# Sums of the MLP's weight factors made early, and the SSD scores masked and summed in PSUM

## The chip, the cores and the metric

The kernel runs on one core of a Trainium2 chip. The metric is the device time of one execution in microseconds (us); three runs of the kernel before gave 3295.22, 3295.41 and 3297.82 us. PE is the matrix engine (TensorE), DVE the vector engine, ACT the scalar engine, POOL the GpSimd engine, SP the engine that only issues transfers. PSUM is the memory that PE writes its products to (eight banks of 512 float32 columns here), SBUF the working memory.

## The reference, cut to what matters

One layer over 2048 tokens plus 16 learned ones, 1024 wide, float32:

```python
z, xbc, dt_raw, u_s5, gates = split(rmsnorm(h) @ w_in)
y_a = ssd_branch(z, xbc, dt_raw, ...)     # scores = C B^T, masked, times decay, times x
y_b = s5_branch(u_s5, ...)                # scan, then y @ w_glu, val * sigmoid(gate)
h = h + (sigmoid(g_a) * y_a + sigmoid(g_b) * y_b) @ w_out
h = h + square(relu(rmsnorm(h) @ w_ff_in)) @ w_ff_out
out = rmsnorm(h)
```

The change touches the inner product of `ssd_branch` (the scores, their mask and the sum over a chunk) and the weights of the two MLP products.

## The kernel before, in words

Every float32 product is made of three matmuls on numbers split into a high and a low part (`mm3`, lines 240 to 246: high x high, high x low, low x high). A split is one ACT copy and one subtraction on DVE or POOL.

**Mixers.** Four blocks of 512 tokens (`b` = 0 to 3). A block has an SSD stage (four groups of four chunks of 128 tokens, beside the dense products that feed them; in block 0 also the S5 scan) and then a tail: the gate products, four GLU groups of two weight units each and two output groups of four units each (`rhs_group`, 16 units in all). In block 0 a unit is loaded raw (512 KB, `wst`), split and written to memory (1 MB, `wsd`); the later blocks load the finished 1 MB units (`wu<-wsd`) on POOL's queue, with three buffers. A group keeps four PSUM banks (`pd`), one for each 128 tokens; DVE empties them (lines 1265 to 1267 in the GLU, 1300 in the output), and only then does PE reuse them. In the trace GLU and output products run from 583 to 685, from 965 to 1065, from 1344 to 1444 and from 1732 on, in block 3 with the MLP's first preparations between GLU (to 1780) and output.

**One chunk of the SSD stage.** `Ssd.front` makes the scores `psc` (three matmuls), masks them into an SBUF tile `smask` (line 836), multiplies the decays `csb` by them (line 838) and splits the result into `mh` and `ml`. `Ssd.back` multiplies `mh` by the high and low halves of `xhl` in one matmul of 128 columns (line 852) and `ml` by the high half in one of 64 (line 854), for each of four heads; DVE adds the two sets of columns with two instructions (line 863). There are 64 such chunks.

**MLP.** Tokens go in three blocks (768, 768, 512). Both products use a Strassen form with seven factors: four sums are made of the four quarters of each pair of raw weight units, and the sums and three quarters themselves are split. There are 32 such groups (8 `di` x 4). In the first block `Weights.make` does all of it: per group two raw loads of 512 KB, four sums on POOL (lines 1369 to 1372, 1383 to 1386), seven splits (`weight`, lines 1344 and 1345: ACT copy, DVE or POOL subtraction) into `wc` tiles, of which there are three, and seven stores of 512 KB to `wcd` on SP (line 1346). The two later blocks only load the finished factors from `wcd`. The first block's products are recorded from 1840 to 2427, the second's from 2440 on.

The order on each engine is planned from a simulated timeline; `tc.issue_after(mm)` keeps instructions from being put ahead of the matmul `mm`. Each engine and each queue then works strictly in its planned order.

Of the kernel before, what the change touches and what calls it, by code (L numbers as in the profile page):

```python
# [9 lines left out]
F32 = mybir.dt.float32  # L10
F32R = mybir.dt.float32r
AF = mybir.ActivationFunctionType
ALU = mybir.AluOpType
# [23 lines left out]
NWC = 5  # L37
NWU = 3
NJK = 1
AHEAD = 1  # L40
NRAW = 4
FPACE = 2
# [85 lines left out]
def _body(ctx, tc, d, out):  # L128
# [63 lines left out]
    tabd = dr.tile([P, NQ, 2, KA + 1], F32, name="tabd")  # L192
    h2d = dr.tile([SEQ, D], F32, name="h2d")
    xtd = dr.tile([7, P, 4, FB[1][1] // 2], F32, name="xtd")
    wcd = dr.tile([8 * 28, P, D], F32, name="wcd")
    csd = dr.tile([NB, NC4 * NH, P], F32, name="csd")
    ud = dr.tile([NM + SEQ, 512], F32, name="ud")
# [51 lines left out]
    def row_scale(ss, rs, n, L=P):  # L249

        V.tensor_scalar(ss[:L, :n], ss[:L, :n], 1.0 / D, EPS, op0=ALU.mult, op1=ALU.add)
        G.tensor_tensor(rs[:L, :n], ss[:L, :n], mhalf[:L, :n], op=ALU.pow)  # L252
# [522 lines left out]
    class Ssd:  # L775
# [47 lines left out]
        def front(self, c):  # L823

            pl, sd, g, x = self.pl, self.sd, self.g, self.ck[c]
            x.cs_ = cs_ = slice(sd.t0 + c * P, sd.t0 + (c + 1) * P)
            self.inputs(x, self.dts, c * NH + g * 4, cs_, P)
            x.dx = pl.tile([P, 4, 64], F32, name="dx", tag="dx", bufs=2)
            V.tensor_tensor(x.dx, x.pth, drow[:, g * 4:g * 4 + 4].unsqueeze(2).broadcast_to([P, 4, 64]), op=ALU.mult)
            x.xhl = pl.tile([P, 4, 2, 64], F32R, name="xhl", tag="xhl", bufs=2)  # L830
            S.copy(x.xhl[:, :, 0, :], x.xdt)
            G.tensor_tensor(x.xhl[:, :, 1, :], x.xdt, x.xhl[:, :, 0, :].bitcast(F32), op=ALU.subtract)
            psc = bank("psc")
            mm3(psc[:, 0:P], sd.bh[:, cs_], sd.bl[:, cs_], sd.ch[:, cs_], sd.cl[:, cs_], True, True)
            sm = pl.tile([P, P], F32, name="smask", tag="smask", bufs=2)
            V.tensor_tensor(sm, psc[:, 0:P], tri, op=ALU.mult)
            csb = self.dec[:, c]
            V.tensor_tensor(csb, csb, sm.unsqueeze(1).broadcast_to([P, 4, P]), op=ALU.mult)
            x.mh = pl.tile([P, 4, P], F32R, name="mh", tag="mh", bufs=2)
            x.ml = pl.tile([P, 4, P], F32R, name="ml", tag="ml", bufs=2)  # L840
            S.copy(x.mh, csb)
            V.tensor_tensor(x.ml, csb, x.mh.bitcast(F32), op=ALU.subtract)

        def back(self, c):

            pl, sd, g, x, dts = self.pl, self.sd, self.g, self.ck[c], self.dts
            i0, cs_ = c * NH + g * 4, x.cs_
            py, po = bank("py"), bank("pyo")
            mm3(po[:, 0:256], sd.ch[:, cs_], sd.cl[:, cs_], self.hh, self.hl, True, True)
            pyv = py.rearrange("p (h a q) -> p h a q", h=4, a=2)  # L850
            for h in range(4):
                T.matmul(pyv[:, h].rearrange("p a q -> p (a q)"), x.mh[:, h, :],
                         x.xhl[:, h].rearrange("p a q -> p (a q)"), start=True, stop=False)
                T.matmul(pyv[:, h, 0, :], x.ml[:, h, :], x.xhl[:, h, 0, :], start=False, stop=True)
            self.update(x, sd.bth[:, c, :], sd.btl[:, c, :], dts.cd, i0, P)
            if c < NC4 - 1:
                self.split()
            x.y = y = pl.tile([P, 4, 64], F32, name="y_", tag="y_", bufs=2)
            for h in range(4):
                V.scalar_tensor_tensor(y[:, h, :], po[:, h * 64:h * 64 + 64], dts.E[:, i0 + h:i0 + h + 1],  # L860
                                       x.dx[:, h, :], op0=ALU.mult, op1=ALU.add)
            for a in range(2):
                V.tensor_tensor(y, y, pyv[:, :, a, :], op=ALU.add)

        def gate(self, c):

# [13 lines left out]
    def decays(pl, dts, g, b):  # L880

        t = pl.tile([P, NC4, 4, P], F32, name="csb", tag="csb", bufs=2 if b else 1)
        src = csd[b].rearrange("(c h) l -> c h l", h=NH)[:, g * 4:g * 4 + 4, :]
        nc.sync.dma_start(t, src.unsqueeze(0).broadcast_to([P, NC4, 4, P]))
        for c in range(NC4):
            for h in range(4):
                i = c * NH + g * 4 + h
                V.tensor_scalar(t[:, c, h, :], t[:, c, h, :], dts.cs[:, i:i + 1], 0.0, op0=ALU.subtract, op1=ALU.min)
        S.activation(t, t, AF.Exp)
        return t  # L890


    xp = pool("xn", stack=xp_st)
# [195 lines left out]
    for b in range(NB):  # L1089
# [166 lines left out]
            xn = make_xn(gp, b + 1, xp)  # L1256
        mh = gp.tile([P, 8, TB], F32R, name="mixh")
        ml = gp.tile([P, 8, TB], F32R, name="mixl")
        for q in range(4):
            n = q // 2  # L1260

            def evac_glu(c, p):
# [4 lines left out]
                V.scalar_tensor_tensor(th, sgbs[n][:, c, o:o + 256], 1.0, th, op0=ALU.add, op1=ALU.mult)  # L1267
                ma = mixA[:, c, q * 256:(q + 1) * 256]
                G.tensor_tensor(ma, ma, th, op=ALU.add)
            rhs_group([(b, U_GLU + q * 2 + i) for i in range(2)], y5h, y5l, evac_glu)  # L1270
            if q % 2 == 0:
                continue
            for c in range(NC4):
# [6 lines left out]
                S.activation(oh, pv, AF.Copy, scale=0.25)  # L1280
                V.scalar_tensor_tensor(ol, pv, 0.25, oh.bitcast(F32), op0=ALU.mult, op1=ALU.subtract)
        if b == NB - 1:
            y5_st.close()
            mp_st.close()
            xp_st.close()
# [9 lines left out]
        for n in range(2):  # L1295
            def evac_out(c, p, n=n, b=b):
# [5 lines left out]
                jk = gp.tile([P, 512], F32, name="jk", tag="jk", bufs=2)  # L1302
                i = b * NC4 + c
                S.activation(jk, xr, AF.Square, accum_out=ssh[:, n, i:i + 1])
            rhs_group([(b, U_OUT + n * 4 + i) for i in range(4)], mh, ml, evac_out)
        if b < NB - 1:
            V.tensor_tensor(ssh[:, 0, b * NC4:(b + 1) * NC4], ssh[:, 0, b * NC4:(b + 1) * NC4],
                            ssh[:, 1, b * NC4:(b + 1) * NC4], op=ALU.add)
            row_scale(ssh[:, 0, b * NC4:(b + 1) * NC4], rsh[:, b * NC4:(b + 1) * NC4], NC4)
        g_st.close()  # L1310
        if b < NB - 1:
            y5_st.close()
# [13 lines left out]
    class Weights:  # L1326
# [14 lines left out]
        def weight(self, w, eng, n, i):  # L1341

            t = wcs[0].tile([P, 2, n, 512 // n], F32R, name="wc", tag="wc", bufs=wcs[1])
            S.copy(t[:, 0], w)
            (V if eng == "v" else G).tensor_tensor(t[:, 1], w, t[:, 0].bitcast(F32), op=ALU.subtract)  # L1345
            nc.sync.dma_start(wcd[i], t.rearrange("p a k n -> p (a k n)").bitcast(F32))
            return t

        def read(self):
# [6 lines left out]
                    yield t.rearrange("p (a k n) -> p a k n", a=2, k=4 if j < 14 else 2)  # L1356

        def make(self):
            for di in range(ND):
                for half in range(2):  # L1360
                    c = 2 * di + half
                    wa, wb = ff_raw(fw, "w1a"), ff_raw(fw, "w1b")
                    nc.sync.dma_start(wa, d["w"][U_FFI + 2 * c])
                    nc.sync.dma_start(wb, d["w"][U_FFI + 2 * c + 1])
                    a11, a12, a21, a22 = [x.rearrange("p (a k n) -> p a k n", a=2, k=4)[:, i]
                                          for x in (wa, wb) for i in range(2)]
                    s2, s3, s1, s4 = [ff_sum(fw, nm).rearrange("p (k n) -> p k n", k=4)
                                      for nm in ("s2", "s3", "s1", "s4")]
                    G.tensor_tensor(s1, a21, a22, op=ALU.add)
                    G.tensor_tensor(s2, s1, a11, op=ALU.subtract)  # L1370
                    G.tensor_tensor(s3, a11, a21, op=ALU.subtract)
                    G.tensor_tensor(s4, a12, s2, op=ALU.subtract)
                    for j, (w, e) in enumerate(zip((a11, s2, s3, a12, s1, a22, s4), ENG[half])):
                        yield self.weight(w, e, 4, di * 28 + half * 7 + j)
                for n in range(2):
                    b1, b2 = ff_raw(fw, "w2a"), ff_raw(fw, "w2b")
                    nc.sync.dma_start(b1, d["w"][U_FFO + 4 * di + n])
                    nc.sync.dma_start(b2, d["w"][U_FFO + 4 * di + 2 + n])
                    b11, b12, b21, b22 = [x.rearrange("p (k a n) -> p k a n", k=2, a=2)[:, :, i, :]
                                          for x in (b1, b2) for i in range(2)]  # L1380
                    t3, t1, t2, t4 = [ff_sum(fw, nm).rearrange("p (k n) -> p k n", k=2)
                                      for nm in ("t3", "t1", "t2", "t4")]
                    G.tensor_tensor(t3, b22, b12, op=ALU.subtract)
                    G.tensor_tensor(t1, b12, b11, op=ALU.subtract)
                    G.tensor_tensor(t2, b22, t1, op=ALU.subtract)
                    G.tensor_tensor(t4, b21, t2, op=ALU.subtract)
                    for j, (w, e) in enumerate(zip((b11, t3, b21, t4, t1, t2, b22), ENG[2 + n])):
                        yield self.weight(w, e, 2, di * 28 + 14 + n * 7 + j)

        def take(self):  # L1390
            ahead = AHEAD if wcs[0] is fw and self.n == 0 else NRAW + wcs[1] - 2
# [373 lines left out]
```

## Time and profile before

| | before |
|---|---|
| median of 3 runs | 3295.41 us |
| profiled execution | 3295.92 us (span 3294.2) |
| PE busy | 3079.3 us (93%) |
| DVE busy | 2082.6 us (63%) |
| POOL busy | 1423.9 us (43%) |
| ACT busy | 1224.1 us (37%) |
| granted clock, mean | 0.97 |
| moved by DMA | 782.9 MB, 238 GB/s |

"Busy" is the share of the span in which an engine had an instruction at work. The granted clock is PE's, as a share of 2.4 GHz. A wait is charged to what came last.

### The profile page before, as it was taken

The page shows a single profiled execution, that of the slowest core. Times are in us where ns is not written, and L with a number is a line of the kernel's source. Part 1 is how long each engine was busy: PE and PEld are TensorE (multiplying, and loading weights), DVE is VectorE, ACT ScalarE, POOL GpSimd, SP SyncE. Part 2 cuts the span into 40 slices and gives each one's busy share as a digit, 9 for nine tenths or more (in the row PEclk, how much of TensorE's full clock was granted, in tenths as well). Part 3 has the DMA queues.
Part 4 walks back from the last instruction along what each step waited for, and adds up shares of the span by engine and source line. Part 5 has one row for each costly group of instructions (what it writes and reads, how often), then busy time and mean ns, then how long its engine had stood idle before and what let it go on. Part 6 is the DMA issues. An engine that isn't in the chain of part 4 may idle for free. (4 is left out here: it accounts for less than half of the span.)

```text
span 3294.2 us, 49794 instructions
## 1 busy us (share of the span) xinstructions
PE 3079.3 (93%) x18353; PEld 2749.2 (83%) x18353; DVE 2082.6 (63%) x4153; ACT 1224.1 (37%) x2428; POOL 1423.9 (43%) x1736
## 2 busy tenths in 40 slices
PE   7898999999999999998999899998879999989998
PEld 6687888877887778877888798888879999989998
DVE  8969997427742576426855566676775555575555
ACT  6254454434431443334433333343442121142222
POOL 4356666524421344213433565656642222243443
PEclk9999999999999999999999899999989999999999
DMA  6486676775556554666756777777788888889998
GB/s 219 146 244 191 198 201 219 271 241 164 168 200 215 185 169 159 209 210 203 233 175 217 271 272 261 264 270 256 271 290 275 247 246 245 249 286 374 358 359 277
DMA packets 297875, 782.90 MB, mean 238 GB/s; under 512 B 90688, under 2 KB 132800, under 8 KB 268448
## 3 DMA queue, kind: packets, MB, share of 16 engines
q0 software_dynamic: 88832, 411.21, 37.5%
q1 hardware_dynamic: 206192, 367.29, 34.1%
q8 instruction: 146, 2.39, 0.3%
q10 hardware_dynamic: 2608, 1.22, 0.1%
q14 instruction: 97, 0.79, 0.1%
HBM read 563.66 MB, written 218.05 MB: 237 GB/s over the span
## 5 line engine op out<-in xcount | busy, mean ns | idle before, releaser
L1504 DVE TENSOR_TENSOR acc<-acc,p 128x512 f32<-128x512 f32 x330 | 225.8, 684 | 172.7 <-PE p L246 169.9
L244 PE MATMUL pd<-hnh,wc 128*128 128x384 f32 (+1 forms) x896 | 293.9, 329 | 29.1 <-DMA wc<-wcd 20.6
L244 PE MATMUL pd<-wu,xnh 128*128 128x512 f32 x768 | 311.1, 406 | 2.3 <-ACT cacc L749 1.6
L245 PE MATMUL pd<-wu,xnh 128*128 128x512 f32 x768 | 310.6, 404 | 0.0
L246 PE MATMUL pd<-wu,xnl 128*128 128x512 f32 x768 | 309.2, 403 | 0.0
L246 PE MATMUL pd<-hnh,wc 128*128 128x384 f32 (+1 forms) x896 | 291.9, 329 | 13.6 <-DVE wc L1345 12.2
L245 PE MATMUL pd<-hnl,wc 128*128 128x384 f32 (+1 forms) x896 | 292.8, 327 | 0.0
L228 POOL DMA_DIRECT2D wu<-wsd x168 | 96.5, 574 | 369.5 <-PE pd L246 305.4
L1355 POOL DMA_DIRECT2D wr<-wcd x227 | 122.4, 540 | 275.2 <-PE pd L246 137.1
L244 PE MATMUL pd<-xnh,wu 128*128 128x512 f32 (+1 forms) x640 | 232.2, 363 | 8.4 <-DMA wu<-wsd 8.4
L246 PE MATMUL pd<-xnh,wu 128*128 128x512 f32 (+1 forms) x640 | 229.6, 359 | 0.0
L245 PE MATMUL pd<-xnl,wu 128*128 128x512 f32 (+1 forms) x640 | 229.5, 359 | 0.0
L1355 POOL DMA_DIRECT2D wc<-wcd x221 | 118.9, 538 | 252.7 <-PE pd L246 134.4
L244 PEld LDWEIGHTS pd<-hnh,wc 128*128 128x128 f32 x896 | 174.3, 195 | 34.0 <-ACT hnh L993 12.9
L246 PEld LDWEIGHTS pd<-hnh,wc 128*128 128x128 f32 x896 | 174.0, 194 | 19.1 <-DVE wc L1345 15.7
L752 DVE SCALAR_TENSOR_TENSOR cacc<-craw,conv,cacc 128x512 f32<-128x512 f32 (+1 forms) x192 | 173.7, 906 | 23.1 <-ACT cacc L749 14.8
L218 POOL TENSOR_TENSOR wu<-wst,wu 128x1024 fp32r<-128x1024 f32 x56 | 138.3, 2471 | 100.0 <-ACT wu L217 98.6
L244 PEld LDWEIGHTS pd<-wu,xnh 128*128 128x128 f32 x768 | 147.0, 191 | 34.8 <-ACT cacc L749 2.4
L245 PEld LDWEIGHTS pd<-hnl,wc 128*128 128x128 f32 x896 | 174.7, 195 | 0.0
L245 PEld LDWEIGHTS pd<-wu,xnh 128*128 128x128 f32 x768 | 147.2, 192 | 31.7 <-issue 0.2
L246 PEld LDWEIGHTS pd<-wu,xnl 128*128 128x128 f32 x768 | 146.9, 191 | 31.8
L244 PEld LDWEIGHTS pd<-xnh,wu 128*128 128x128 f32 x640 | 125.1, 196 | 25.3 <-ACT cacc L749 3.6
(1016 smaller groups left out, 9910.3 us busy)
## 6 DMA issues: line engine op xcount, KB each, us to landing
wu<-wsd POOLq DMA_DIRECT2D x168, 1024.0 KB, 5.2
wr<-wcd POOLq DMA_DIRECT2D x227, 512.0 KB, 5.0
wcd<-wc SPq DMA_DIRECT2D x224, 512.0 KB, 3.5
wc<-wcd POOLq DMA_DIRECT2D x221, 512.0 KB, 5.3
wsd<-wu SPq DMA_DIRECT2D x56, 1024.0 KB, 5.3
wst<-in_w SPq DMA_DIRECT2D x60, 512.0 KB, 5.7
csb<-csd SPq DMA_DIRECT2D x16, 1024.0 KB, 12.0
xt<-in_x SPq DMA_DIRECT2D x28, 512.0 KB, 4.7
```

Source lines behind the costliest of these rows:

```text
L218: eng.tensor_tensor(t[:, 1], raw, t[:, 0].bitcast(F32), op=ALU.subtract)
L228: nc.gpsimd.dma_start(t, wsd[u - U_XBC])
L244: T.matmul(ps, lh, rh, start=first, stop=False, skip_group_check=open_)
L245: T.matmul(ps, lh, rl, start=False, stop=False, skip_group_check=open_)
L246: return T.matmul(ps, ll, rh, start=False, stop=last, skip_group_check=open_).ins
L752: V.scalar_tensor_tensor(acc[:, :n], raw[:, k:k + n], conv[:, mt, k:k + 1], acc[:, :n], op0=ALU.mult, op1=ALU.add)
L1355: nc.gpsimd.dma_start(t, wcd[di * 28 + j])
L1504: V.tensor_tensor(o, o, pv, op=ALU.add)
```

## The change

In the tail of each mixer block a generator, `ff_early`, takes 9, 9, 9 and 5 of the 32 groups of MLP weights: it loads the two raw units, makes the four sums on DVE and stores them, not split, to a new memory tensor `smd` (256 KB each). `early_step` spreads them over the tail's 16 units (in block 3 over the GLU's 8), behind the last matmul of a unit. `Weights.make` no longer makes sums: it loads them (five buffers) and loads of one raw unit of each pair only the half that it still splits; the next group's raw loads are issued behind the first factor of this one. In the SSD stage the mask is applied in place in PSUM, and the two halves of `x` are accumulated into one set of 64 columns with three matmuls of 64 columns for each head, so that one DVE addition is left.

```diff
+EARLY = (9, 9, 9, 5)
...
-            sm = pl.tile([P, P], F32, name="smask", tag="smask", bufs=2)
-            V.tensor_tensor(sm, psc[:, 0:P], tri, op=ALU.mult)
+            sm = psc[:, 0:P]
+            V.tensor_tensor(sm, sm, tri, op=ALU.mult)
...
-            pyv = py.rearrange("p (h a q) -> p h a q", h=4, a=2)
+            pyv = py[:, 0:256].rearrange("p (h q) -> p h q", h=4)
             for h in range(4):
-                T.matmul(pyv[:, h].rearrange("p a q -> p (a q)"), x.mh[:, h, :],
-                         x.xhl[:, h].rearrange("p a q -> p (a q)"), start=True, stop=False)
-                T.matmul(pyv[:, h, 0, :], x.ml[:, h, :], x.xhl[:, h, 0, :], start=False, stop=True)
+                mm3(pyv[:, h], x.mh[:, h, :], x.ml[:, h, :], x.xhl[:, h, 0, :], x.xhl[:, h, 1, :], True, True)
...
-            for a in range(2):
-                V.tensor_tensor(y, y, pyv[:, :, a, :], op=ALU.add)
+            V.tensor_tensor(y, y, pyv, op=ALU.add)
...
+    def ff_early(pl, groups):
+        def load(g):
+            wa, wb = [pl.tile([P, D], F32, name=nm, tag="er", bufs=2) for nm in ("era", "erb")]
+            ff_load(g, wa, wb)
+            return wa, wb
+        raw = load(groups[0])
+        for n, g in enumerate(groups):
+            v, m = ff_pieces(g, *raw)
+            def room(nm):
+                return pl.tile([P, 512], F32, name=nm, tag="es", bufs=4).rearrange("p (k n) -> p k n", k=m)
+            for j, w in ff_sums(g, v, room, V):
+                nc.sync.dma_start(smd[g * 4 + SUMS[m].index(j)], w.rearrange("p k n -> p (k n)"))
+                if j == (6 if m == 4 else 3) and n + 1 < len(groups):
+                    raw = load(groups[n + 1])
+                yield
...
+        slots = 8 if b == NB - 1 else 16
+        early_n = [0, 0]
+        def early_step(mm):
+            early_n[0] += 1
+            want = -(-early_n[0] * EARLY[b] * 4 // slots)
+            with tc.issue_after(mm):
+                while early_n[1] < want:
+                    early_n[1] += 1
+                    next(early, None)
...
-            rhs_group([(b, U_GLU + q * 2 + i) for i in range(2)], y5h, y5l, evac_glu)
+            rhs_group([(b, U_GLU + q * 2 + i) for i in range(2)], y5h, y5l, evac_glu, step=early_step)
...
-            rhs_group([(b, U_OUT + n * 4 + i) for i in range(4)], mh, ml, evac_out)
+            rhs_group([(b, U_OUT + n * 4 + i) for i in range(4)], mh, ml, evac_out, step=early_step if b < NB - 1 else None)
...
         def make(self):
-                    G.tensor_tensor(s1, a21, a22, op=ALU.add)
-                    G.tensor_tensor(s2, s1, a11, op=ALU.subtract)
-                    G.tensor_tensor(s3, a11, a21, op=ALU.subtract)
-                    G.tensor_tensor(s4, a12, s2, op=ALU.subtract)
...
+            def load_sum():
+                g, k = next(more, (None, 0))
+                if g is not None:
+                    t = ff_sum(fw, "sm")
+                    nc.sync.dma_start(t, smd[g * 4 + k])
+                    sums.append(t)
+            load_raws(0)
+            for _ in range(NSUM):
+                load_sum()
+            for g in range(32):
+                (a11, a12, a21, a22), m = ff_pieces(g, *raws.pop(0))
+                ws = {0: a11, 3: a12, 5: a22} if m == 4 else {0: a11, 2: a21, 6: a22}
+                for j in range(7):
+                    w = ws[j] if j in ws else sums.pop(0).rearrange("p (k n) -> p k n", k=m)
+                    t = self.weight(w, ENG[g % 4][j], m, g * 7 + j)
+                    if j not in ws:
+                        load_sum()
+                    if j == 0 and g < 31:
+                        load_raws(g + 1)
+                    yield t
```

## Rows read from the trace of the kernel before

**Rows 1.** The page's part 2: granted clock and DMA rate in 40 equal slices.
```profile
PEclk9999999999999999999999899999989999999999
GB/s 219 146 244 191 198 201 219 271 241 164 168 200 215 185 169 159 209 210 203 233 175 217 271 272 261 264 270 256 271 290 275 247 246 245 249 286 374 358 359 277
```

**Rows 2.** Busy time by stretch: stretch, length, engines, granted clock, DMA share, GB/s.
```profile
1840.00:2427.00 587.00, 525.36 (x3397) 505.72 (x3396) 405.99 (x564) 234.13 (x431) 353.09 (x260) 0.95 0.74 270
2520.00:2890.00 370.00, 369.13 (x2585) 367.88 (x2584) 201.54 (x346) 76.22 (x151) 104.83 (x186) 1.00 0.81 247
```

**Rows 3.** PE's waits from 1840 to 2427: us in total, times, longest.
```profile
PE p L244 <- DVE acc L1504: 14.0, 7, 2.8
PE pd L246 <- DVE wc L1345: 12.2, 7, 2.1
PE py L244 <- DVE acc L1504: 8.1, 6, 1.4
PE p L245 <- POOL wc L1345: 6.6, 7, 1.9
PE px L244 <- DVE acc L1514: 6.4, 5, 1.5
PE p L244 <- ACT wc L1344: 5.4, 7, 1.4
PE pd L244 <- ACT wc L1344: 4.6, 8, 2.1
```

**Rows 4.** All engines' waits from 1840 to 2427, three of the longest.
```profile
ACT wc L1344 <- DMA wcd<-wc: 115.1, 81, 4.1
POOL t L1383 <- DMA w2b<-in_w: 62.9, 12, 6.8
...
POOL s L1369 <- DMA w1b<-in_w: 32.2, 12, 5.1
```

**Rows 5.** POOL's groups from 1840 to 2427: costliest and last of eight sum lines.
```profile
L1384 POOL TENSOR_TENSOR t<-w2a 128x512 f32<-128x512 f32 x16 | 25.2, 1576 | 0.6 <-DVE wc L1345 0.6
...
L1369 POOL TENSOR_TENSOR s<-w1b 128x512 f32<-128x512 f32 x14 | 18.7, 1338 | 41.3 <-DMA w1b<-in_w 32.2 <-DMA wcd<-wc 5.1 <-DVE acc L1504 4.0
```

**Rows 6.** Busy time by stretch, the tails of blocks 0, 1 and 3.
```profile
583.00:685.00 102.00, 101.33 (x475) 81.14 (x474) 40.66 (x64) 38.45 (x66) 46.85 (x32) 1.00 0.75 270
965.00:1065.00 100.00, 100.00 (x470) 80.40 (x469) 34.65 (x63) 23.99 (x50) 20.64 (x32) 1.00 0.58 199
...
1732.00:1780.00 48.00, 48.00 (x219) 38.50 (x219) 18.06 (x37) 11.66 (x26) 15.28 (x24) 1.00 0.57 197
```

**Rows 7.** Busy time by stretch, twenty of the MLP's last block.
```profile
3000.00:3020.00 20.00, 20.00 (x168) 19.89 (x167) 14.76 (x34) 7.64 (x20) 9.34 (x16) 1.00 1.10 389
```

**Rows 8.** DMA issues, from issue to landing: page's part 6; 2500:2880; 3000:3250.
```profile
wst<-in_w SPq DMA_DIRECT2D x60, 512.0 KB, 5.7
...
wr<-wcd POOLq DMA_DIRECT2D x100, 512.0 KB, 4.5
...
wr<-wcd POOLq DMA_DIRECT2D x76, 512.0 KB, 5.6
```

**Rows 9.** PE in order of time (start, duration): scores, then sums of a chunk.
```profile
774.82 0.28 PE L245 MATMUL psc<-cl,bh 128*128 128x128 f32 x1
774.93 0.27 PE L246 MATMUL psc<-ch,bl 128*128 128x128 f32 x1
775.04 0.45 PE L246 MATMUL pd<-wu,xnl 128*128 128x512 f32 x1
...
812.28 0.31 PE L852 MATMUL py<-xhl,mh 128*128 128x128 f32 x1
812.42 0.25 PE L854 MATMUL py<-xhl,ml 128*128 128x64 f32 x1
812.50 0.30 PE L852 MATMUL py<-xhl,mh 128*128 128x128 f32 x1
```

**Rows 10.** DVE's groups over the span; the last row is a pair of L863 (64 pairs).
```profile
L1504 DVE TENSOR_TENSOR acc<-acc,p 128x512 f32<-128x512 f32 x330 | 225.8, 684 | 172.7 <-PE p L246 169.9 <-DMA out<-acc 0.8 <-DMA acc<-h2d 0.7
L838 DVE TENSOR_TENSOR csb<-csb,smask 128x512 f32<-128x512 f32 x64 | 73.1, 1149 | 1.0
...
L863 DVE TENSOR_TENSOR y__3031<-y__3031,py x2: 404/406/408, 273.6 to 276.4; 128x256 f32<-128x256 f32 x2
```

**Rows 11.** Busy time by stretch, the SSD stages of blocks 0 and 1.
```profile
192.00:565.00 373.00, 345.62 (x2073) 298.38 (x2072) 334.34 (x650) 190.72 (x415) 247.11 (x245) 0.95 0.70 201
765.00:965.00 200.00, 194.55 (x975) 161.78 (x974) 133.72 (x309) 79.91 (x169) 89.26 (x132) 0.98 0.54 176
```

More of the change, by code (lines that the diff above doesn't have):

```diff
@@ L39 @@
 NJK = 1
+EARLY = (9, 9, 9, 5)
+SUMS = {4: (1, 2, 4, 6), 2: (1, 3, 4, 5)}
 AHEAD = 1
@@ L194, in _body @@
     xtd = dr.tile([7, P, 4, FB[1][1] // 2], F32, name="xtd")
+    smd = dr.tile([32 * 4, P, 512], F32, name="smd")
     wcd = dr.tile([8 * 28, P, D], F32, name="wcd")
@@ L890, in decays, with ff_pieces, ff_load, ff_sums @@
         return t
+    def ff_pieces(g, wa, wb):
+        if g % 4 < 2:
+            v = [x.rearrange("p (a k n) -> p a k n", a=2, k=4)[:, i] for x in (wa, wb) for i in range(2)]
+            return v, 4
+        v = [x.rearrange("p (k a n) -> p k a n", k=2, a=2)[:, :, i, :] for x in (wa, wb) for i in range(2)]
+        return v, 2
+    def ff_load(g, wa, wb):
+        di, j = divmod(g, 4)
+        ua, ub = (U_FFI + 4 * di + 2 * j, U_FFI + 4 * di + 2 * j + 1) if j < 2 else \
+            (U_FFO + 4 * di + j - 2, U_FFO + 4 * di + j)
+        nc.sync.dma_start(wa, d["w"][ua])
+        nc.sync.dma_start(wb, d["w"][ub])
+    def ff_sums(g, v, room, eng):
+        a11, a12, a21, a22 = v
+        def tt(nm, x, y, op):
+            o = room(nm)
+            eng.tensor_tensor(o, x, y, op=op)
+            return o
+        if g % 4 < 2:
+            s1 = tt("s1", a21, a22, ALU.add)
+            yield 4, s1
+            s2 = tt("s2", s1, a11, ALU.subtract)
+            yield 1, s2
+            yield 2, tt("s3", a11, a21, ALU.subtract)
+            yield 6, tt("s4", a12, s2, ALU.subtract)
+        else:
+            yield 1, tt("t3", a22, a12, ALU.subtract)
+            t1 = tt("t1", a12, a11, ALU.subtract)
+            yield 4, t1
+            t2 = tt("t2", a22, t1, ALU.subtract)
+            yield 5, t2
+            yield 3, tt("t4", a21, t2, ALU.subtract)
+    def ff_split(t, w, eng, i):
+        S.copy(t[:, 0], w)
+        eng.tensor_tensor(t[:, 1], w, t[:, 0].bitcast(F32), op=ALU.subtract)
+        nc.sync.dma_start(wcd[i], t.rearrange("p a k n -> p (a k n)").bitcast(F32))
+    def ff_early(pl, groups):
[13 more added lines that the diff above has]
+                yield
     xp = pool("xn", stack=xp_st)
@@ L1258, in _body @@
         ml = gp.tile([P, 8, TB], F32R, name="mixl")
+        e_st = ExitStack()
+        g0 = sum(EARLY[:b])
+        early = ff_early(pool("early%d" % b, stack=e_st, side="right"), range(g0, g0 + EARLY[b]))
+        slots = 8 if b == NB - 1 else 16
[7 more added lines that the diff above has]
+                    next(early, None)
         for q in range(4):
@@ L1282, in _body @@
         if b == NB - 1:
+            for _ in early:
+                pass
+            e_st.close()
             y5_st.close()
@@ L1309, in _body @@
             row_scale(ssh[:, 0, b * NC4:(b + 1) * NC4], rsh[:, b * NC4:(b + 1) * NC4], NC4)
+        for _ in early:
+            pass
+        e_st.close()
         g_st.close()
@@ L1343, in weight @@
             t = wcs[0].tile([P, 2, n, 512 // n], F32R, name="wc", tag="wc", bufs=wcs[1])
-            S.copy(t[:, 0], w)
-            (V if eng == "v" else G).tensor_tensor(t[:, 1], w, t[:, 0].bitcast(F32), op=ALU.subtract)
-            nc.sync.dma_start(wcd[i], t.rearrange("p a k n -> p (a k n)").bitcast(F32))
+            ff_split(t, w, V if eng == "v" else G, i)
             return t
@@ L1358, in make @@
         def make(self):
[L1359 to L1368, printed above, removed]
-                    G.tensor_tensor(s1, a21, a22, op=ALU.add)
-                    G.tensor_tensor(s2, s1, a11, op=ALU.subtract)
-                    G.tensor_tensor(s3, a11, a21, op=ALU.subtract)
-                    G.tensor_tensor(s4, a12, s2, op=ALU.subtract)
[L1373 to L1388, printed above, removed]
@@ new lines, in make, with load_raws @@
+            raws, sums = [], []
+            more = ((g, k) for g in range(32) for k in range(4))
+            def load_raws(g):
+                di, j = divmod(g, 4)
+                a, b = [ff_raw(fw, nm) for nm in ("wa", "wb")]
+                if j < 2:
+                    u = U_FFI + 4 * di + 2 * j
+                    nc.sync.dma_start(a, d["w"][u])
+                    nc.sync.dma_start(b[:, 512:], d["w"][u + 1][:, 512:])
+                else:
+                    u = U_FFO + 4 * di + j - 2
+                    nc.sync.dma_start(a.rearrange("p (k a n) -> p k a n", k=2, a=2)[:, :, 0, :],
+                                      d["w"][u].rearrange("p (k a n) -> p k a n", k=2, a=2)[:, :, 0, :])
+                    nc.sync.dma_start(b, d["w"][u + 2])
+                raws.append((a, b))
```

## The prediction

> **What bounds the kernel now.** I read the slices first [rows 1]. PE is at work 93% of the span, so only time in which PE stands still or runs at the lower clock can be won, and every matmul that is added in a full stage is paid. The clock row and the busy times by stretch show where that time lies. In the second MLP block PE is full at clock 1.00; in the first, which does the same products, it is busy 525.4 of 587 us at 0.95 [rows 2]. At the second block's rate (2585 recorded matmuls in 370 us, 6.99 per us) the first's 3397 would take 486 us: it loses 101 us. Of these 587 - 525.4 = 61.6 are idle; a mean of 0.95 means that a tenth of the stretch, some 59 us, ran at 1.2 GHz, which loses 29. The four tails, where the sums go, are the opposite: PE full at clock 1.00, with DVE busy only 35 to 41 of 100 us and 197 to 270 GB/s moving [rows 6]. The SSD stages are nearly full (PE 194.6 of 200 in block 1), but in block 0 DVE is at 90% and PE at 93%, clock 0.95 [rows 11].
>
> Second, the waits in the first MLP block [rows 3, 4]. PE waits for late DVE additions (14.0 + 8.1 + 6.4), for weight splits on DVE (12.2) and POOL (6.6), for ACT's copies (5.4 + 4.6). Behind these stand two things: POOL, whose queue stops for raw loads in front of its sums (62.9 + 32.2 us) while splits lie behind them; and the ring of three `wc` tiles, in which ACT waits 115.1 us, 81 times, until a store to `wcd` has landed. The change takes away the first. It does not touch the second.
>
> **Part 1: the first MLP block.** POOL loses 128 sums of 1.34 to 1.58 us [rows 5], some 181 of its 353 busy us. DVE is helped too: a DVE instruction with two SBUF inputs has a mean of 1149 ns where one with an input in PSUM takes 684 [rows 10], and the difference is best read as waiting for POOL. What goes: the POOL waits (7), half of the DVE waits (12.2 + 28.5 = 41, half because POOL's busy time about halves), together 28; and the clock that goes with them, 29 x 28/62 = 13. That is 41 us. The raw loads are no longer late, since they are issued seven factors (some 17 us) ahead and land in about 6.
>
> What comes: each group reads 256 KB less of two raw units and 1 MB of sums, 0.79 MB more, 25 MB over 32 groups. The block now moves 270 x 587 = 158 MB [rows 2]; 184 MB in 550 us would be 334 GB/s. SP issues four more transfers a group, none of which waits for anything that the store ahead of it hasn't waited for. But loads of 512 KB land in 4.5 us at 247 GB/s and in 5.6 at 361 [rows 8]; 64 GB/s more make about 0.6 us, and each `wc` store in the ring gets that later. On 81 waits this is 49 us of ACT; PE now idles 10 of 115 us on ACT directly and more through DVE's splits, so I charge 7. Net -34. Bounds: at 361 GB/s the 184 MB take 509 us, so no more than -78; if PE feels all 49 us of the ring, +8.
>
> **Part 2: the tails.** Each of 32 groups adds 1.05 MB of loads and 1.05 MB of stores: 18.9 MB in blocks 0 to 2, 10.5 MB in block 3. Now 27.5, 19.9, 20.1 (block 2 is like block 1) and 9.5 MB move there [rows 6], so it becomes 46.4, 38.8, 39.0 and 20.0 MB in 102, 100, 100 and 48 us: 455, 388, 390 and 417 GB/s. The most I see over 20 us is 389 [rows 7]. At that rate the tails need at least 119, 100, 100 and 51 us: +20 in all, the lower bound. The Trainium skill's page DMA: Bandwidth & Descriptors (Specifications) puts the limit of memory for one core at about 358 GB/s; by that rule the lower bound would be +52 (+28, +8, +9, +8), but 389 and 361 GB/s were measured here, so I do not use it.
>
> The upper side is the chain of one group, which has only two raw buffers: loads, sums, stores, and only then the next loads. Two loads: 5.7 us for one [rows 8] and 1.35 more for the second's bytes at 389 GB/s, 7.0. Four sums at 0.69 us (the price of a 512-column addition, rows 10; up to 1.15 beside POOL), 2.8. The stores lie ahead of the next loads in SP's queue, 2.7 us of transfer of which up to 2.1 run beside the sums: 0.6 to 2.7. Together 10.4 to 12.5 us, against 11.1 us that a tail has for one group (9.6 in block 3). With half of the bandwidth taken by the other queue the loads cost 2.7 more and it is 15. DVE works in its planned order, so while it waits for a raw unit it does not empty banks; SP likewise holds `xr` loads and `h2d` stores behind, and in block 0 the raw units of the dense products. I take 12.5, and 14 in block 0, whose own traffic is heavier: 9 x 14 - 102 = 24; twice 9 x 12.5 - 100 = 12.5; 5 x 12.5 - 48 = 14.5; 63.5 us. PE has some 4.5 us in hand in each tail (three quarters of a unit of 6 us) before it needs a bank: 63.5 - 18 = +46. Bounds +20 and, at 15 us a group, 33 + 35 + 35 + 27 - 18 = +112. The sums' DVE time itself (36 x 0.69 = 25 us a tail) fits beside its 35 to 41.
>
> **Part 3: the SSD chunks.** PE gets 12 matmuls of 64 columns for a chunk instead of four of 128 and four of 64. The trace has no run of 64-column matmuls. Start to start, matmuls of 128 columns with changing weights take 0.11 us, and the pair of a 128 and a 64 takes 0.22 (812.28 to 812.50), 0.14 of it behind the 128 and 0.08 behind the 64 [rows 9]. If each costs 0.11 whatever its columns, four more make 0.44 us a chunk, 28 us over 64; if a 64 costs 0.08, three make 0.24 for 0.22, 5 us in all. I take 0.11, since the 0.22 of a pair is twice that. The Trainium skill's page TensorE: Matmul & The Clock Gate (LDWEIGHTS) says that a weight load takes the weights' columns over 1.2 in ns, which for 128 is 107 ns however few columns follow; by that rule it is 27 us, by the cheap reading 5.
>
> DVE loses one addition (0.41) and, with the mask in PSUM, perhaps 1149 - 684 = 0.47 of the multiplication [rows 10]: 0.87 us a chunk. In block 0, where DVE limits, 16 chunks give 14 us for 7 of PE: -7. In the other three 48 x 0.44 = +21 is paid on a nearly full PE, and at best the waits of 5.5 us a block [rows 11] halve: +14 with 7 off. Sum +7, bounds -20 and +25. The masked scores hold their bank some 1.5 us longer; four such banks turn, and I price that at nothing; if a transposition waits for it, it costs up to that per chunk in block 0 alone, 24 us.
>
> **The sum.** -34 + 46 + 7 = +19. The profiled execution took 3295.9, 0.5 above the median of the runs; 3295.4 + 19 = 3314 us.
>
> **Rivals.** (a) Faster: POOL was the root in the first MLP block, the ring was late only through it, and the block comes within 30 us of the second's rate (-70), while the plan hides the chains of the tails down to their bytes (+22): with part 3, -41, 3254 us. For it: 95 us of POOL's waits on raw loads in front of splits. Against: the 115 us of ACT on stores. It decides as soon as the block wins over 53. (b) Part 3 is good: 64-column matmuls are cheap and DVE was the limit: -20 instead of +7, 3287 us, about no change. (c) The change doesn't do what it says: POOL is freed, but the ring of three with later stores keeps the first MLP block where it was: 46 + 7, 3348 us. (d) The tails fall to 15 us a group: 112 + 7 - 34, 3380 us; the clock would then fall there too.
>
> **How the numbers follow.** Forecast 0.38, (a) 0.31, (b) 0.12, (c) 0.13, (d) 0.06. A measurement of this kernel tells 0.2%, 6.6 us, from no change. Faster: (a) and 0.05 of (b), 0.36. Same: 0.05 of (b) and 0.04 from the forecast's edge, 0.09. Slower: 0.55. The cases of both signs are likely; the forecast's own range is 3300 to 3335, and the range that holds 8 in 10 reaches from (a) to (d): 3250 to 3380.
>
> **What would show it.** Part 1: POOL's waits for `w2b` and `w1b` gone, PE busy over 92% and clock above 0.96 in the first MLP block, ACT still waiting for `wcd` stores over 100 us, about 340 GB/s; block some 550 us. Part 2: the tails of 100 us at 110 or more, over 350 GB/s, DVE waiting for `era` or `erb`, PE for DVE in front of `pd`, clock below 1.00. Part 3: eight gaps of 0.9 us become twelve of 1.3; the multiplication near 684 ns. Wrong outright: a first MLP block under 515 us, or tails that stay at 100 us.

## The result and the profile after

The changed kernel takes 3333.15 us (median of four runs, 3326.03 to 3345.93) against 3296.61 for the kernel before in the same comparison: 1.0113 times as long, 95% interval 1.0081 to 1.0145, so 36.5 us slower. The forecast was 3314. The profiled execution is the fastest of the four, 3326.03 us (span 3324.3). The stages below therefore explain 30 us; the other 6 belong to executions that left no trace.

A stage is taken from the first product of one part to the first of the next, in both traces; only the tails of blocks 0 to 2 and the first MLP block end with their own last product. What PE stands still behind such a product counts in the next stage: 3.5 us behind the first tail of the changed kernel, a wait for a `wu` load, are part of the +11.8.

| stage | before, us | after - before, us | forecast |
|---|---|---|---|
| start to the first tail (S5, SSD of block 0) | 583.2 | -2.3 | -7 |
| SSD stages of blocks 1, 2, 3 | 847.5 | +11.8, +3.6, +7.0 | +14 together |
| tails of blocks 0, 1, 2 | 301.0 | +19.7, +17.9, +17.0 | +46 with the next row |
| GLU of block 3 (the last tail) | 47.7 | +4.5 | |
| output of block 3, preparation | 61.0 | -1.9 | 0 |
| first MLP block | 586.3 | -38.3 | -34 |
| the rest | 867.5 | -8.9 | 0 |

The tails cost 59, the SSD stages 20; the MLP gives 38 back, and 9 more at the start of its second block. Page part 2 of after, clock and DMA rate in 40 slices:

```profile
PEclk9999999999999999999999999999999999999999
...
GB/s 218 147 244 193 209 203 229 354 288 192 154 229 317 234 169 159 246 336 235 185 197 255 285 329 339 338 329 327 341 313 291 250 247 247 247 282 373 361 358 278
```

Three tails stand out as new peaks (354, 317, 336), and the first MLP block moved from about 266 to about 333 [rows 1]. The same by stretch (length; busy time of PE, weight load, DVE, ACT, POOL; clock, DMA share, GB/s), for the four tails and the first MLP block of after, then the first tail in thirds:

```profile
581.00:702.00 121.00, 106.68 (x472) 83.35 (x471) 59.14 (x96) 38.07 (x65) 49.18 (x33) 0.94 0.95 366
994.00:1112.00 118.00, 106.51 (x472) 83.46 (x471) 54.21 (x96) 24.50 (x51) 21.71 (x32) 0.96 0.89 311
1395.00:1512.00 117.00, 104.56 (x470) 81.98 (x469) 54.81 (x96) 24.23 (x51) 20.94 (x32) 0.97 0.88 311
1806.00:1859.00 53.00, 51.20 (x225) 40.37 (x224) 25.22 (x52) 12.71 (x27) 15.33 (x23) 0.97 0.91 321
1917.00:2466.00 549.00, 507.24 (x3399) 491.10 (x3399) 350.90 (x566) 234.21 (x433) 184.94 (x140) 0.98 0.93 335
...
581.00:620.00 39.00, 29.80 (x129) 23.68 (x128) 21.59 (x35) 13.44 (x23) 12.22 (x8) 0.82 0.87 324
620.00:660.00 40.00, 40.00 (x191) 31.10 (x190) 26.91 (x47) 15.23 (x29) 23.98 (x18) 1.00 0.98 376
660.00:702.00 42.00, 36.89 (x156) 28.57 (x155) 10.63 (x17) 9.41 (x16) 12.99 (x7) 1.00 1.01 394
```

PE was full at 1.00 in these tails [rows 6]. Now it is idle for 14.3, 11.5, 12.4 and 1.8 us, 40 in all. A mean clock of 0.94 to 0.97 means that 12, 8, 6 and 6% of the stretches ran at 1.2 GHz, 34 us in all. In 7 of these PE stood still anyway, and the other 27 lose half of their time, some 14 us. Together about 54 of the 59 us. DVE stays at half load, so it isn't the engine that is full. The DMA engines nearly are: their share is 0.88 to 0.95 where it was 0.57 to 0.75.

### The profile page after: what moved, and what is told of

It is laid out like the page before. It is cut to its first block, busy times and chain, and to the rows that moved or that the text cites. A ratio compares the mean times of both kernels' runs of the same rounds, so it can differ in the third digit from the quotient of the medians.

```text
span 3324.3 us, 50855 instructions
## 1 busy us (share of the span) xinstructions
PE 3107.3 (93%) x18609; PEld 2770.4 (83%) x18609; DVE 2044.2 (61%) x4217; ACT 1220.6 (37%) x2426; POOL 1220.7 (37%) x1608
## 5 line engine op out<-in xcount | busy, mean ns | idle before, releaser
L247 PE MATMUL pd<-xnh,wu 128*128 128x512 f32 (+1 forms) x640 | 231.2, 362 | 12.3 <-DMA wu<-wsd 12.1
L247 PEld LDWEIGHTS pd<-hnh,wc 128*128 128x128 f32 x896 | 172.0, 192 | 26.3 <-issue 17.0
L755 DVE SCALAR_TENSOR_TENSOR cacc<-craw,conv,cacc 128x512 f32<-128x512 f32 (+1 forms) x192 | 165.7, 865 | 25.9 <-ACT cacc L752 14.7
L247 PEld LDWEIGHTS pd<-xnh,wu 128*128 128x128 f32 x640 | 124.0, 194 | 29.6 <-issue 11.8
```

What stands on the lines that cost most here:

```text
L247: T.matmul(ps, lh, rh, start=first, stop=False, skip_group_check=open_)
L755: V.scalar_tensor_tensor(acc[:, :n], raw[:, k:k + n], conv[:, mt, k:k + 1], acc[:, :n], op0=ALU.mult, op1=ALU.add)
```

## The experiments

Times are medians, ratios are to the kernel before on the same chip with their 95% interval, stage times from the profiled execution against before's.

**1. The three parts apart.** The sums alone are after with the old mask and the old two sets of columns; the other three kernels are before with one or both edits of the SSD chunk:

```diff
-            sm = pl.tile([P, P], F32, name="smask", tag="smask", bufs=2)
-            V.tensor_tensor(sm, psc[:, 0:P], tri, op=ALU.mult)
+            sm = psc[:, 0:P]                            # mask in PSUM
+            V.tensor_tensor(sm, sm, tri, op=ALU.mult)
...
+                mm3(pyv[:, h], x.mh[:, h, :], x.ml[:, h, :], x.xhl[:, h, 0, :], x.xhl[:, h, 1, :], True, True)   # y in one set
...
+            V.tensor_tensor(y, y, pyv, op=ALU.add)
```

> The early sums alone; scores masked into SBUF and y in two sets of columns as before. Theory: the tails cost about 59 us, the first MLP block gives back 38 and what follows 9, and the SSD stages are as before, so 3296 + 12 = 3308 us, SSD stages within 4 us of before. Rival (the 20 us that the SSD stages lost are a spill of the early transfers into them, not the four added matmuls): 3326 us, SSD stages 15 to 20 us longer than before.

> The SSD edits alone, no early sums. Theory: 64 chunks x 0.44 us of matmul is 28 us on PE, less what DVE's relief saves, some 8: 3296 + 20 = 3316 us, with twelve matmuls of 64 columns 0.11 us apart. Rival (spill): PE's added matmuls hide behind waits, no slower than before, 3290 to 3297 us.

> The mask in PSUM alone. Theory: the multiplication falls from 1149 to 690 ns, 29 us of DVE; PE gets nothing more, so only the waits on DVE shrink: -4 to -10 us, 3290 us. Rival (the scores' bank held longer delays PE, or the time of DVE was not on the path): 3296 or some us more.

> y in one set of columns alone: four more matmuls and one DVE addition less for each of 64 chunks. Theory: +28 us of PE, less 26 us of DVE that were mostly beside PE: +20 to +25, 3318 us. Rival (matmuls of 64 columns are cheap or hide): 3290 to 3300 us.

| kernel | us | ratio | stages against before |
|---|---|---|---|
| sums alone | 3322.25 | 1.0087 (1.0063 to 1.0112) | tails and GLU 3 +20.4, +17.2, +22.4, +4.3; output 3 +4.3; MLP -46.9 |
| mask and y | 3311.68 | 1.0053 (1.0034 to 1.0072) | SSD of blocks 0 to 3 -1.6, +8.2, +4.2, +7.8 |
| mask alone | 3283.43 | 0.9971 (0.9957 to 0.9984) | SSD -6.2, -0.6, -3.5, -2.0 |
| y alone | 3315.40 | 1.0070 (1.0048 to 1.0093) | SSD +3.3, +10.0, +5.4, +7.6 |

The parts add up within their intervals: 27 and 17 make 44, measured 36.5. Mask and y came close to what was expected. The sums alone, expected at 3308, cost 14 us more; their profiled execution (3314.88 us) shows half of that, in the tails and the output. Their SSD stages stayed within 6 us of before, so the rival that the early transfers spill into these stages falls. The edits of the chunk have opposite signs. y alone costs 26.3 us in the stages, almost the 28 of its matmuls: the DVE addition that it saves is worth some 2. (The total of y alone is smaller, because its first MLP block, in which nothing was changed, came out 12 us shorter in the profiled execution; one stage of one execution can be off by that much.) The mask alone gains 12.3 in the stages, and it is the best version here, faster than both kernels. Its mechanism is one row, DVE's multiplication with the mask alone (busy us, mean ns | idle before), which was 1149 ns with the mask's product in SBUF [rows 10]:

```profile
L838 DVE TENSOR_TENSOR csb<-csb,psc 128x512 f32<-128x512 f32 x64 | 43.2, 681 | 1.1
```

The single instructions show what the 1149 were made of. Before, the 12 multiplications with no POOL instruction at work beside them took 681 ns in the mean, the other 52 1257; with the mask's product in PSUM it was 680 for 15 and 682 for 49 (the spans on POOL are rough). So this multiplication was slow where POOL worked beside it, and the operand in PSUM took that away.

And PE in order of time (start, duration) in a chunk of after shows the price of 64 columns, which no row of before had:

```profile
799.65 0.28 PE L247 MATMUL py<-xhl,mh 128*128 128x64 f32 x1
799.76 0.28 PE L248 MATMUL py<-xhl,mh 128*128 128x64 f32 x1
799.88 0.28 PE L249 MATMUL py<-xhl,ml 128*128 128x64 f32 x1
799.99 0.28 PE L247 MATMUL py<-xhl,mh 128*128 128x64 f32 x1
```

They start 0.11 us apart, as matmuls of 128 columns do [rows 9]. The Trainium skill's page TensorE: Matmul & The Clock Gate (LDWEIGHTS), which the prediction weighed, gives 107 ns for a weight load of 128 columns by its rule; the trace agrees.

**2. What makes the tails long: the chain of two raw buffers, DVE's sums, or the bytes.** Three kernels, each from the sums alone: four raw buffers of each name with the next group loaded ahead; the raw loads of a tail's first group only (the later sums are made of old data); and no sums on DVE, with the raw pieces stored in their place, so the transfers are the same.

```diff
-            wa, wb = [pl.tile([P, D], F32, name=nm, tag="er", bufs=2) for nm in ("era", "erb")]
+            wa, wb = [pl.tile([P, D], F32, name=nm, tag="er", bufs=4) for nm in ("era", "erb")]
...
-                    raw = load(groups[n + 1])
+                    pass
...
-            for j, w in ff_sums(g, v, room, V):
-                nc.sync.dma_start(smd[g * 4 + SUMS[m].index(j)], w.rearrange("p k n -> p (k n)"))
+            for k, j in enumerate((4, 1, 2, 6) if m == 4 else (1, 4, 5, 3)):
+                w = raw[k // 2][:, (k % 2) * 512:(k % 2) * 512 + 512]
+                nc.sync.dma_start(smd[g * 4 + SUMS[m].index(j)], w)
```

> The early sums alone (as e1_sums_only), with four raw buffers instead of two: a group's raw units are loaded before the sums of the group ahead. Bytes are the same. Chain theory (a tail is paced by load, sums, stores, load): tails fall from 20 us above before to 0 to 8, 3322 - 45 = 3277 us. Rate theory (388 to 455 GB/s are more than the queues give, so buffers do not help): tails stay 15 us or more above, 3312 to 3325 us.

> The early sums alone, but in each tail only the first group's raw units are loaded and summed again for every group: 8 of 9 MB of loads are left out, and with them what a sum waits for; sums and stores stay. Both DMA theories: tails within 5 us of before, 3322 - 55 = 3267 us. Rival (the 36 sums' own time on DVE delays the banks): tails stay 12 us or more above, 3305 us or more.

> The early sums alone, but DVE makes none: quarters of the raw units are stored in place of the sums, so loads, stores and bytes are the same and the sums' values are left out. If the delay reaches PE through DVE standing before a raw unit, tails fall to 0 to 8 us above before, 3280 us. If it reaches PE through the transfers of the dense work (wu, xr, yt late for want of bandwidth or behind on SP's queue), they stay 12 us or more above, 3310 us.

| kernel | us | ratio | tails 0, 1, 2 and GLU 3 against before |
|---|---|---|---|
| sums alone | 3322.25 | 1.0087 (1.0063 to 1.0112) | +20.4, +17.2, +22.4, +4.3 |
| four raw buffers | 3323.83 | 1.0077 (1.0062 to 1.0092) | +25.2, +13.4, +11.7, +2.0 (SSD 3: +17) |
| few raw loads | 3291.91 | 0.9983 (0.9971 to 0.9995) | +18.2, +4.7, +6.0, +7.6 |
| no sums on DVE | 3324.61 | 1.0078 (1.0055 to 1.0101) | +17.5, +14.0, +17.0, +10.4 |

The chain falls: with twice the buffers the total stays, and what tails 1 and 2 and GLU 3 win comes back in SSD 3 and tail 0; tails 1 and 2 still lose 25 of 40 us. DVE falls: without one sum the tails are still 59 us longer. Taking away 8.4 of the 18.9 MB wins tails 1 and 2 nearly back, but not tail 0, and the total misses the expected 3267 by 25 us. By stretch, tails 0 and 1 with few raw loads:

```profile
586.00:706.00 120.00, 107.28 (x473) 83.99 (x471) 67.91 (x97) 38.82 (x67) 52.21 (x33) 0.94 0.84 305
991.00:1095.00 104.00, 100.73 (x468) 80.10 (x467) 54.92 (x96) 23.96 (x51) 22.15 (x32) 1.00 0.79 273
```

At 273 GB/s PE is 97% busy at 1.00; at 305, in block 0, it is not. So in blocks 1 and 2 the raw loads are most of the price, and in block 0 there is something more.

**3. Only the bytes.** Before with unread loads of 512 KB on SP's queue: 36 in each of tails 0 to 2 and 20 in the last, the change's own 18.9 and 10.5 MB, with no sum, no store and the MLP as it was.

```diff
+                    t = dlp.tile([P, D], F32, name="dead", tag="dead", bufs=4)
+                    nc.sync.dma_start(t, d["w"][U_FFI + dn[1]])
```

> The kernel before, with as many bytes added to each tail as the early sums move (36, 36, 36 and 20 loads of 512 KB on SP into four buffers that nothing reads), and nothing else: no sums, no stores, MLP as before. Bytes theory: the tails cost 40 to 65 us as with the sums, 3335 to 3355 us, PE waiting for wu and xr. Rival (not the bytes but SP's queue, standing before stores that wait for sums, and the sums' place on DVE): tails +20 or less, 3315 us at most.

It took 3366.15 us, 1.0226 (1.0209 to 1.0243); tails +24.3, +10.8, +9.2 and GLU 3 +8.1, 52 in sum where the change lost 59, and SSD 3 +12 more, which stays unexplained. By stretch, the start of tail 0, the whole of it, and tails 1 and 2:

```profile
583.00:620.00 37.00, 21.63 (x78) 16.25 (x77) 8.41 (x15) 9.32 (x15) 6.83 (x5) 0.72 1.02 405
583.00:709.00 126.00, 108.91 (x478) 85.16 (x477) 38.50 (x65) 40.31 (x68) 48.69 (x33) 0.92 0.94 356
992.00:1103.00 111.00, 103.64 (x473) 82.59 (x472) 35.16 (x64) 23.91 (x51) 20.57 (x32) 0.98 0.88 331
1383.00:1492.00 109.00, 101.37 (x471) 80.42 (x470) 34.06 (x64) 23.93 (x51) 20.52 (x32) 1.00 0.89 334
```

The sum agrees better than its parts. Tail 0 and GLU 3 lose more than in the change; tails 1 and 2 lose 20 us where the change loses 35, although more is moved in each us (331 and 334 GB/s, in the change 311), and 8 of their 36 loads are issued ahead of the tail. So the bytes alone bring the loss, but equal bytes do not bring an equal one. Half of the change's bytes are stores, each behind a sum; no run takes this difference apart.

What PE waits for in tail 0 (us in total, times, longest):

```profile
PE y5p L1246 <- ACT yt L1243: 13.0, 2, 7.4
```

And the DMA issues of its first 37 us (KB each, median us from issue to landing):

```profile
dead<-in_w SPq DMA_DIRECT2D x16, 512.0 KB, 5.3
wsd<-wu SPq DMA_DIRECT2D x2, 1024.0 KB, 11.3
wst<-in_w SPq DMA_DIRECT2D x2, 512.0 KB, 12.2
yt<-yd SPq DMA_DIRECT2D x2, 256.0 KB, 11.1
```

This is what is special in block 0: 16 of the 36 loads are issued in these 37 us, the DMA engines are full at 405 GB/s, and the 256 KB `yt` loads, from which the operand of the GLU products is still being made (`y5p`, `y5h`), land after 11.1 us. PE stands, and its mean clock there is 0.72. The change shows the same wait (below).

**4. Another place, another queue.** The sums moved into the SSD stages of blocks 1 to 3 (with the mask in PSUM); the early loads and stores on ACT's queue; and that with the mask in PSUM.

```diff
-EARLY = (9, 9, 9, 5)
+EARLY = (0, 11, 11, 10)       # the steps now follow the SSD stage's units
...
-        nc.sync.dma_start(wa, d["w"][ua])
+        nc.scalar.dma_start(wa, d["w"][ua])       # likewise wb and the stores to smd
```

> A version drawn from the runs: the sums of 11, 11 and 10 groups are made in the SSD stages of blocks 1 to 3 (32 units long, 176 to 202 GB/s now), none in the tails; mask in PSUM, y as before. If the tails' cost was that their transfers were already dense: MLP -47, mask -10, SSD stages +0 to +20 for 30 sums' time on DVE: 3240 to 3260 us. Rival (the price of the early transfers is the same anywhere): 3295 us or more.

> The early sums alone, their loads and stores issued on ACT's queue, so that xr, yt, wst and wsd have SP's queue for themselves. Bytes theory: tails stay 45 us or more above, 3310 to 3325 us (ACT held by the waits could add to it). Queue theory: block 0's tail, whose raw units and yt come over SP, falls by 10 us or more and the others by some 5, 3290 to 3300 us.

> As e10_act_queue, with the mask in PSUM. The effects add: 7 to 12 us below e10 (the mask alone gave 9.7), whatever e10 shows; under the queue theory 3285 us, faster than both kernels; under the bytes theory 3305 us.

In the SSD stages: 3346.21 us, 1.0150 (1.0129 to 1.0170), a clear miss. SSD 1 to 3 grew by 19, 25 and 17 us. The plan also pulled sums forward into the tails ahead (first stores at 645, in block 0's tail), so tails 0 to 2 stayed 9 to 16 us longer than before: the two places were not separated, but no cheap place was found. On ACT's queue: 3364.46 us, 1.0219 (1.0192 to 1.0245), 42 more than on SP's. In tail 0 ACT is now the engine that is held (us in total, times, longest):

```profile
POOL wu L221 <- ACT wu L220: 39.2, 6, 11.4
```

With the mask it took 3343.23 us, 1.0153 (1.0135 to 1.0170): 21 less, where 7 to 12 were expected. Tails and GLU 3 were +27.8, +19.0, +31.1 and +13.2 on ACT's queue, each longer than on SP's, so both theories missed. Freeing SP's queue did not shorten a tail, but since ACT is held in its place, the run doesn't rule that queue out.

**5. Was it enough to load earlier?** The mask alone, and in the first MLP block the next group's raw loads issued behind the first factor; the sums stay on POOL and no byte is added.

```diff
+                for j in range(7):
+                    t = self.weight(ws[j], ENG[g % 4][j], m, g * 7 + j)
+                    if j == 0 and g < 31:
+                        load_raws(g + 1)
```

> The kernel before with the mask in PSUM (e3_mask_only) and, in the first MLP block, the next group's two raw loads issued behind the first factor of this group, as the change does, but the sums made on POOL as before and no early sums: no byte is added. If POOL's standing before raw loads (63 + 32 us) was the root of what the first MLP block gained, the block takes 550 to 570 us instead of 587 and the kernel 3283 - 25 = 3258 us. If it was the sums' own 181 us on POOL (and what DVE loses to them), the block stays above 580 us and the kernel at 3280 to 3286 us.

It took 3287.31 us, 0.9983 (0.9973 to 0.9993): no better than the mask alone, the first MLP block at 585.7, as the second alternative had it. The waits show why this doesn't settle the question (us in total, times, longest):

```profile
ACT wc L1344 <- DMA wcd<-wc: 102.4, 75, 4.1
POOL t L1384 <- DMA wb<-in_w: 70.5, 12, 13.1
```

POOL waits for the second raw unit as before [rows 4]: its buffer is read until the last factors of the group ahead, so the load can't start earlier (one pair: `wa` issued at 2083.6, `wb` at 2101.8). The wait was not removed, and whether it alone held the block stays open.

## Why the prediction was right, and where it was not

**Direction and form: right.** The prediction had the MLP block win less than the tails and the chunks lose, and that is what happened: -38 and -9 against +59 and +20. Its sum was half of the slowdown, because two terms were too small, by 13 us each, against 13 that the MLP won beyond its term. The median lies at the upper end of the forecast's own range, 3300 to 3335, and two of the four executions lie beyond it.

**Part 1, -34 forecast, -38 measured.** Both halves of the sum hold. PE's idle time fell from 61.6 us to 549 - 507.2 = 41.8, 20 less (28 for the waits less 7 for the ring were charged). The clock rose from 0.95 to 0.98, so the loss at 1.2 GHz fell from 29 us to about 11 (4% of 549, halved), 18 less (13 charged). But other waits went than I said. PE's waits in the first MLP block of after (us in total, times, longest):

```profile
PE p L248 <- DVE wc L935: 14.7, 25, 0.7
PE p L247 <- ACT wc L934: 11.0, 9, 2.7
PE p L248 <- POOL wc L935: 5.8, 8, 2.2
...
PE p L247 <- DVE acc L1594: 2.0, 1, 2.0
```

All engines' waits there, of ACT and POOL:

```profile
POOL wc L935 <- ACT wc L934: 279.2, 91, 15.6
ACT wc L934 <- DMA wcd<-wc: 154.5, 105, 4.6
...
POOL wc L935 <- DMA sm<-smd: 32.2, 6, 10.2
```

And DVE's split of a sum (busy us, mean ns | idle before):

```profile
L935 DVE TENSOR_TENSOR wc<-sm,wc 128x512 fp32r<-128x512 f32 x71 | 48.8, 687 | 34.9 <-ACT wc L934 29.8 <-DMA wcd<-wc 5.0
```

Against [rows 3] the late DVE additions nearly all went (28.5 to 2.0), where I had halved them. The splits stayed (DVE 14.7, POOL 5.8, ACT 11.0), where I had let POOL's go. DVE's split of a sum takes 687 ns; before it took 1034 in the mean for `s` and 902 for `t`, while a split of a raw quarter took 703:

```profile
L1345 DVE TENSOR_TENSOR wc<-s,wc 128x512 fp32r<-128x512 f32 x39 | 40.3, 1034 | 38.6 <-ACT wc L1344 33.3 <-DMA wcd<-wc 4.9 <-DMA w1b<-in_w 0.3
L1345 DVE TENSOR_TENSOR wc<-w1a,wc 128x512 fp32r<-128x512 f32 x15 | 10.5, 703 | 5.0 <-ACT wc L1344 5.0
```

So it isn't POOL's share of the stretch (60%, then 34%) as such that made them slow, but POOL at work beside them: of the 40 splits of an `s` in the whole trace of before, the 16 with no POOL instruction at work beside them took 687 ns in the mean, the other 24 1295. DVE is now done sooner with each such piece, and the best reading is that it comes to its additions earlier for that. POOL's new 32 us of waits for sums harm no one that the trace shows. The ring grew as forecast, ACT's wait from 115.1 to 154.5 us, at 335 GB/s. Rival (c), that the ring keeps the block where it was, falls; a fourth `wc` tile was not tried. Of the remaining 42 us of idle time 33 lie behind the splits, and the ring is the longest wait of ACT, whose copies come first. How much of the 38 us is due to the sums gone from POOL and how much to the earlier loads was not taken apart.

**The rest, 0 forecast, -9 measured.** The second block's first products wait for a factor to be read back; that wait fell from 12.7 to 5.7 us, and with it the clock of its first 100 us rose from 0.88 to 0.93. PE's wait before, then after:

```profile
PE pd L244 <- DMA wc<-wcd: 12.7, 1, 12.7
...
PE pd L247 <- DMA wc<-wcd: 5.7, 1, 5.7
```

It was 11 to 13 us in every other kernel without early sums. I had read this block only from 2520 on [rows 2] and so missed its start.

**Part 2, +46 forecast, +59 measured.** The step that failed is the chain, "Together 10.4 to 12.5 us": the two raw buffers do not set a group's time (four left the total as it was), and DVE, which did wait for `erb` as forecast (18 us in the first tail, 31 in the second), is not held to any harm (no sums changed nothing). That the first tail came out as forecast, 24 - 4.5 = 19.5 and 19.7 measured, is luck: by the same chain tails 1 and 2 were to lose 8 each and lost 17.9 and 17.0, GLU 3 was to lose 10 and lost 4.5. What counts is the transfers themselves, 52 us in sum when nothing but unread loads is added, though not tail by tail. The lower bound of +20 spread the bytes evenly at the most that 20 us had shown [rows 7]. But the transfers are not spread: four stores to `smd` are issued at 574 to 578, ahead of the first tail's first product, and the rates of the thirds above are 324, 376 and 394 GB/s. So the hold behind a unit's last matmul did not spread them over the units as the change meant it to. Loads that PE depends on then land later. PE's waits in after's first tail:

```profile
PE y5p L1309 <- ACT yt L1306: 8.5, 2, 4.9
PE pd L248 <- POOL wu L221: 3.0, 2, 1.7
```

The four `yt` loads of a block share one buffer: the next is issued when PE has transposed the one before, so their delays add up. The last two of these transpositions, before and after (start, duration, idle before):

```profile
588.81 0.60 PE L1245 MATMUL y5p<-ident,yt 128*128 128x128 f32 x4
593.25 0.60 PE L1245 MATMUL y5p<-ident,yt 128*128 128x128 f32 x4
...
591.52 1.11 PE L1309 MATMUL y5p<-ident,yt 128*128 128x128 f32 x4 [4.85 <-ACT yt L1306]
601.57 1.11 PE L1309 MATMUL y5p<-ident,yt 128*128 128x128 f32 x4 [3.68 <-ACT yt L1306]
```

The last one comes 20.7 us behind the tail's first product instead of 10.1. PE's waits in the second tail:

```profile
PE pd L247 <- DMA wu<-wsd: 4.2, 2, 2.7
PE pd L247 <- DVE xr L1380: 3.7, 1, 3.7
```

And the DMA issues of the second tail (KB each, median us from issue to landing):

```profile
wu<-wsd POOLq DMA_DIRECT2D x16, 1024.0 KB, 7.5
...
smd<-s SPq DMA_DIRECT2D x16, 256.0 KB, 8.4
...
erb<-in_w SPq DMA_DIRECT2D x7, 512.0 KB, 7.9
```

In block 0 it is `yt`, not the `pd` banks that I named; PE waits for it in the first third, whose mean clock is 0.82. In block 1 the `wu` loads take 7.5 us instead of 5.1 and are waited for, though three buffers stand ahead of PE. A later landing alone is not the whole price, though: with few raw loads `wu` took 7.3 us and tail 1 lost only 4.7. So the waits and the clock behind them make up most of the 59 us, and which transfer is late differs by block. The Trainium skill's page DMA: Bandwidth & Descriptors (Specifications) would have given +52 by its 358 GB/s. That lands near in the sum, but not by tail (+28, +8, +9, +8), and 394 GB/s over 42 us and 405 over 37 were moved here, so its limit isn't what was reached. Rival (d), 15 us a group, falls: the tails took about 13 us a group (121, 118 and 117 for nine).

**Part 3, +7 forecast, +20 measured.** The matmuls were priced right: 28 us by rows, 26 net by y alone. The step that failed is DVE's relief: 21 us were credited to the mask and the saved addition, 12 and 2 came when each was changed alone, and some 8 together (28 - 20). The multiplication fell by 0.46 us a chunk as forecast, 30 us over 64, but only 12 of them lay in front of PE, half in block 0. There the forecast was -7 and the two edits together gave -1.6. Rival (b), cheap matmuls of 64 columns, falls.

**Rival (a)**, POOL as the root with the tails hiding their chains, falls: the block won 38 (47 with the rest of the MLP in the sums alone), under the 53 from which it decides, and the tails hid nothing.

**What stays open:** the 6 us between the profiled execution and the median, and why equal bytes cost tails 1 and 2 less as unread loads. That block 0's tail keeps +18 with few raw loads lies for the most part in the same `yt` chain: its last transposition still comes 21.7 us behind the tail's first product, and the first 24 us still move 352 GB/s.

## What to carry to other kernels

Work taken off a crowded engine by way of memory is paid in the stage where the transfers go: add its bytes to that stage's rate and see whether the loads that PE lives on still land in time, since a full PE at clock 1.00 has nothing to give. A matmul of 64 columns cost here what one of 128 does, so count matmuls, not columns. An operand in PSUM can make a DVE instruction with two inputs faster beside a busy POOL, and cost nothing here, where the data were there anyway.

## What the runs showed of the hardware

A small load in a burst of larger ones can cost more than its bytes: with the DMA engines full at 405 GB/s for 37 us, 256 KB took 11.1 us to land, where the same loads took 5.5 in the kernel before. When PE stood still in the crowded tails, the granted clock fell too (0.72 in that stretch, 0.82 in after's first third), and over after's four tails this second loss was about a third of the first (14 us beside 40). It does not follow from every stall: in the third tail with unread loads PE was idle 7.6 of 109 us, at 1.00. A DVE subtraction of two 128x512 operands in SBUF took 687 ns in the mean with no POOL instruction at work beside it and 1295 with one; a multiplication 681 and 1257 with both inputs in SBUF, and 680 and 682 with one in PSUM.
